# Reordering the head of a two-layer diffusion step: modulation blocks, first projection and first norm

## The chip, the core and the metric

The kernel runs on one core of one Trainium2 chip. The metric is the device time of one execution in microseconds (us); before the change it is 1575.97 us, the median of 3 runs (1575.73 to 1576.37).

## What is computed

One inference step of a hybrid diffusion backbone of two layers, with 128 context tokens and 128 latent tokens (256 columns together), model width 1024. Each layer is a SwiGLU feed-forward half step, a token mixer with three branches, and a second feed-forward half step. Only the very beginning matters here:

```
mod = silu(cond) @ w_ada + b_ada          # nine vectors of 1024 per layer and condition
h   = rmsnorm(x, gain) * (1 + scale) + shift
g,u = split(h @ w_in)                     # w_in: 1024 x 5632, width 2816 each
x   = x + 0.5 * gate * ((silu(g) * u) @ w_out)
```

Shift and scale are vectors 0 and 1 of `mod`. All numbers are fp32.

## The kernel before

Activations lie transposed: `x` is 8 chunks of 128 channels by 256 tokens. Every weight tile is 128 x 1024 fp32 (512 KB), loaded into a `raw` buffer (4 of them) by SyncE, cast on ScalarE to a high part (`emit_hi`, line 578; in the trace `wh`, or `big` for the first five tiles) and split on VectorE into a low part (`emit_lo`, line 588, raw minus high; `wl` or `big`). `split` (line 1681) does both for the next tile. `emit_lo` also asks for the next loads. One product of a 128 x 128 weight chunk k with an activation chunk k is three matmuls (high x high, high x low, low x high), called a triple here (`mm3`); eight triples k = 0 to 7 make one output tile. The first projection, feed-forward input of layer 0, takes 44 such tiles. Its first five (`T0 = 5`) are computed in the head, together with the modulation, because their activation operand comes chunk by chunk: three accumulate in the three `pm` buffers of PSUM and two in a spare one (`s` in the trace).

The activations are fed without the norm: `xfeed` (line 828) writes the high and low part of x times gain times (1 + scale) for one chunk, two instructions on ScalarE (`big<-x,amod`) and two on VectorE (`big<-x,amod,big`). The norm's factor per token is multiplied in after the projection, when a PSUM tile is evacuated: `wide<-pm,rb`, where `rb` holds the factor in all rows. It is formed from the sums of squares: `xstat` (line 765) squares a chunk on ScalarE and adds it to `sqa` on VectorE; `rstd_diag` (line 781) sums over partitions on TensorE, takes the power on GpSimd and builds a diagonal on VectorE; `rstd_rows` (line 795) spreads it with one fp32 product and copies it to `rb` on ScalarE. `norm_chain` (line 804) is the two in a row.

The modulation of the first norm comes in eight blocks, two loads of 512 KB each (`big<-wa`). Block b gives shift and scale of chunk b. `block_mm` (line 1699) multiplies silu(cond) with the block on TensorE (`pa<-big,silc`, 16 entries in the trace: the first 8 need the first half of the block, the others the second) and copies the result out on VectorE (`t1k<-pa`). `block_feed` (line 1709) turns that copy into columns on TensorE (`s<-cst,t1k`, 4 entries), adds bias and gain on VectorE (`mods`, `amod`, and two short writes of the shift), and calls `xfeed`.

Each engine works through its instructions in the order in which this Python program issues them. The head of before issues them so: loads of cT (8 KB), x (1 MB), cst and prm (about 130 KB each), then weight tiles 0 and 1, block 0, tile 2, block 1, tile 3, block 2, tile 4; all squares and the whole norm chain; `split` of two tiles; then ten steps. Step s issues `block_mm(s)`, the load of block s + 3, `block_feed(s - 1)`, then the triples of all chunks up to s - 2 for the tiles that have joined (`JOIN`: tiles 0 and 1 at step 2, then one each at steps 3, 4, 5), and a `split` where a tile is about to join. In the last steps high and low parts of tiles 5, 6 and the high part of tile 7 are issued (`AHEAD`, line 82). After the loop `ffn_in` (line 878) evacuates the five tiles and goes on with tile 5 into the first `pm` buffer that is free; its `end` issues the parts of further tiles (five ahead high, four ahead low) behind each evacuation.

Some later side work (the other modulation vectors) is issued by a planner, `Pace`, that predicts when each engine gets to what was issued; only the order of issue rests on it.

Of the kernel before, what the change touches and what calls it, by code (L numbers as in the profile page):

```python
# [17 lines left out]
D = 1024  # L18
# [22 lines left out]

ADA_DEPTH = 2
T0 = 5
JOIN = (0, 0, 3, 4, 5)
RAW_BUFS = 4
WH_BUFS = 5
WL_BUFS = 5
# [29 lines left out]
BR_LESS = (0, 0, 0, 0, 1, 1, 1, 1)  # L77
WO_LESS = (0, 0, 0, 0, 1, 1, 1, 1)
FO_LESS = (0, 0, 0, 0, 1, 1, 1)
LOADS = (2, 3, 4, 4)  # L80
PRE = 2
AHEAD = ("", "hl", "h", "lh", "")
T_SIDE = 3
T_SETUP = 6
YCUT = ((0, 2), (2, 2), (4, 2), (6, 2))
# [243 lines left out]


class Pace:
    """Predicts when each engine gets to what has been issued to it, so that side work can be issued where it waits for
    nothing. Only the order of issue rests on it; every wait is still placed by the tile framework."""

    LAT = {"pe": 0.25, "dve": 0.13, "act": 0.17, "pool": 0.2, "dma": 2.2}

# [91 lines left out]
def backbone(ctx: ExitStack, tc: tile.TileContext, seq, wst, wada, wa0, wrow, xT_d, cT_d, cB_d, ck_d, cv_d, h0_d, prm_d, cst_d,  # L428
# [117 lines left out]
    def settle(cond):  # L546
        idle = 0
        while not cond():
            cand = [(s, lst) for lst, n in ((side["first"], 99), (side["gens"], CONC), (side["slow"], 99)) for s in lst[:n]]
            cand = [c for c in sorted(cand, key=lambda c: when(c[0]) - FIRST * (c[1] is side["first"])) if when(c[0]) < 1e8]  # L550
            idle = 0 if any(step_side(*c) for c in cand) else idle + 1
            assert idle < 3
# [7 lines left out]
    def misc(gen):  # L560
        add(gen, True)
# [5 lines left out]
    def load(out, src):  # L567
        nc.sync.dma_start(out=out, in_=src)
        pace.op("dma", out.free_size() * P * 4 / 360e3, [out], [])

    def load_more(limit):
        while st["load"] < min(limit, st["cap"]):
            i = st["load"]
            raws[i] = pace.slot("raw", RAW_BUFS, wp.tile([P, 1024], F32, tag="raw", bufs=RAW_BUFS, name=nm("raw")))
            load(raws[i], wst[i])
            st["load"] += 1

    def emit_hi():
        u = st["hi"]
        if u < T0:  # L580
            hi = big(F32R)
        else:
            hi = pace.slot("wh", WH_BUFS, wp.tile([P, 1024], F32R, tag="wh", bufs=WH_BUFS, name=nm("wh")))
        S.copy(hi, raws[u])
        wt[u] = [hi, None]
        st["hi"] += 1
# [178 lines left out]
    def xstat(m):  # L765
        if m == 0:
            stat["acc"] = tmp("sqa", [P, NT], bufs=1)
            S.activation(out=stat["acc"], in_=x[:, 0], func=AF.Square)
            return lambda: None
        q = stat["sq"] = t1k()  # L770
        S.activation(out=q, in_=x[:, m], func=AF.Square)
        return lambda: V.tensor_tensor(out=stat["acc"], in0=stat["acc"], in1=q, op=ALU.add)
# [31 lines left out]
    def norm_chain(box):  # L804
        yield "pe", stat["acc"], "s1"
        dg = rstd_diag(stat["acc"], 1.0 / D)
        yield "pe", dg, "s1"
        box["rb"] = rstd_rows(dg)
# [856 lines left out]
        box["done"] = True  # L1665

    load(cT, cT_d)
    load(x, xT_d)
    load(cst[:, 0:CST_E], cst_d[:, 0:CST_E])
    load(prm[0], prm_d[0, :, 0:PRM_R])  # L1670
    V.memset(silc, 0.0)
    V.memset(halfc, -0.5)
    S.activation(out=silc[:, :, 0:2], in_=cT, func=AF.Silu)
# [7 lines left out]
    def split():  # L1681
        emit_hi()
        emit_lo()

    for n in LOADS[:-1]:
        load_more(n)
        block_load()
    load_more(LOADS[-1])
    feed_open(0, 0)
    for m in range(KD):  # L1690
        xstat(m)()
    box = {"rb": None}
    misc(norm_chain(box))
    split()
    split()
    settle(lambda: box["rb"] is not None)
    evs = {}

    def block_mm(b):
        ps = pada()  # L1700
        for k in range(KD):
            j = k % 4
            T_.matmul(ps[32 * j:32 * j + 32, :], lhsT=silc[:, k, :], rhs=blocks[b][k // 4][:, j * NT:(j + 1) * NT],
                      start=(k < 4), stop=(k >= 4))
        evs[b] = t1k()
        V.tensor_copy(evs[b], ps)
        blocks[b] = None
# [18 lines left out]
    spare = ps2()  # L1726
    pre, ws = [], []
    done = {}
    for step in range(KD + 2):
        if step < KD:  # L1730
            block_mm(step)
            if len(blocks) < KD:
                block_load()
                if len(blocks) == KD:
                    st["cap"] = len(seq)
                    load_more(st["lo"] + RAW_BUFS)
        if 1 <= step <= KD:
            block_feed(step - 1)
        for t in range(T0):
            if step < max(2, JOIN[t]):  # L1740
                continue
            if t == len(pre):
                ws.append(tiles8(use(("fin", 0, 0, (t % 2) * KF + t // 2))))
                pre.append(pmain(NT + 2) if t < 3 else spare[:, t - 3, 0:NT + 2])
                done[t] = 0
            while done[t] <= step - 2:
                k = done[t]
                mm3(pre[t], ws[t][k:k + 1], feed["hs"][k:k + 1], k == 0, k == KD - 1)
                done[t] += 1
        if st["lo"] < T0 and step + 2 >= JOIN[st["lo"]]:  # L1750
            split()
        if step >= KD - 3:
            for what in AHEAD[step - KD + 3]:
                what = emit_hi() if what == "h" else emit_lo()
    while st["lo"] < T0 + PRE:
        if st["hi"] == st["lo"]:
            emit_hi()
# [54 lines left out]
```

## Time and profile before

| | |
|---|---|
| median of 3 runs | 1575.97 us |
| profiled execution: span, its own time | 1579.0 us (the page gives no other time of it) |
| PE (TensorE) busy | 1547.9 us, 98% |
| DVE (VectorE) busy | 1313.5 us, 83% |
| ACT (ScalarE) busy | 877.7 us, 56% |
| POOL (GpSimd) busy | 58.7 us, 4% |
| transfers | 349.59 MB, mean 221 GB/s |

PE is the engine of the matmuls; its weight loads overlap. All times below are in us from the start of the span. A row of the timeline is start, duration, engine, line, operation, out<-in with buffer numbers left out, shapes and count; in brackets the idle time of the engine before it and what ended it. L397 is a helper through which all compute instructions are issued, so rows are told apart by their tiles.

### The profile page before, as it was taken

The numbers are of one execution on the slowest core, as the hardware profiler recorded it, in microseconds if no ns is written. First come the engines' busy times: TensorE is split into PE (matmuls) and PEld (weight loads), VectorE is DVE, ScalarE is ACT, GpSimd is POOL, SyncE is SP. The second block draws the span as 40 slices with busy tenths as digits, with TensorE's granted clock in tenths as the row PEclk, the third lists the DMA queues.
The fourth block names the chain that finished last, engine by engine and source line by source line (L and its number), as shares of the span: only waits on it lengthen the run. The fifth ranks groups of instructions, "written<-read, shape, count | busy, mean of one in ns | idle before, by whom it ended". The sixth has DMA issues, their size and how long they took to land.

```text
span 1579.0 us, 31076 instructions
## 1 busy us (share of the span) xinstructions
PE 1547.9 (98%) x12154; PEld 1449.6 (92%) x12154; DVE 1313.5 (83%) x2391; ACT 877.7 (56%) x1640; POOL 58.7 (4%) x65
## 2 busy tenths in 40 slices
PE   6999999999999999999999999999999999999997
PEld 4998889999979999899899998998998999999986
DVE  4777798988598997899989999898768889989754
ACT  3564447676467446644547544576746754665442
POOL 0000002000001100100001000100000010010000
PEclk9999999999999999999999999999999999999998
DMA  9698764553674666687765877555447457557652
GB/s 365 210 336 291 280 247 168 189 174 114 219 241 155 214 241 221 216 300 286 261 221 195 301 268 268 181 187 177 138 146 278 166 206 258 177 200 282 218 181 81
DMA packets 99171, 349.59 MB, mean 221 GB/s; under 512 B 10960, under 2 KB 14672, under 8 KB 98896
## 3 DMA queue, kind: packets, MB, share of 16 engines
q1 hardware_dynamic: 99024, 347.60, 62.4%
q8 instruction: 96, 1.57, 0.4%
q14 instruction: 51, 0.42, 0.1%
HBM read 343.36 MB, written 4.19 MB: 220 GB/s over the span
## 4 chain that ended last, share of the span: by engine, by line
PE 76%; issue 12%; DVE 7%; DMA 3%; ACT 1%; POOL 1%; DVEq 0%; SPq 0%; POOLq 0%; ACTq 0%
PE pm L397 67%; PE s L397 7%; DVE wl L397 2%; DVE big L397 2%; PE pa L397 2%; DMA big<-wada 2%; DVE t1k L397 1%; POOL osr L397 1%; DVE wide L397 0%; DMA t<-prm 0%; DMA x<-xT 0%; ACT big L397 0%; DVE sqa L397 0%; ACT L397 0%; ACT t1k L397 0%
## 5 line engine op out<-in xcount | busy, mean ns | idle before, releaser
L397 PE MATMUL pm<-big,wh 128*128 128x256 f32 (+2 forms) x6568 | 1288.8, 293 | 2.5 <-DVE wide L397 1.6
L397 PEld LDWEIGHTS pm<-big,wh 128*128 128x128 f32 x6568 | 1028.5, 189 | 46.3 <-issue 16.4
L397 PE MATMUL pm<-big,wl 128*128 128x256 f32 (+1 forms) x3592 | 1004.1, 281 | 0.0
L397 PEld LDWEIGHTS pm<-big,wl 128*128 128x128 f32 x3592 | 676.7, 188 | 2.4
L397 DVE TENSOR_TENSOR wl<-raw,wh 128x1024 fp32r<-128x1024 f32 x481 | 586.4, 1224 | 25.3 <-ACT wh L397 25.0
L397 ACT CAST wh<-raw 128x1024 fp32r<-128x1024 f32 x481 | 501.3, 1047 | 135.2 <-PE pm L397 105.4
L397 DVE SCALAR_TENSOR_TENSOR big<-big,big 128x1024 f32<-128x1024 f32 x198 | 241.4, 1219 | 9.7 <-DMA big<-wrow 8.6
L397 ACT CAST big<-t1k 128x256 fp32r<-128x256 f32 x88 | 35.8, 407 | 151.8 <-DVE t1k L397 151.8
L397 ACT ACTIVATE big<-x,amod 128x128 fp32r<-128x128 f32 x96 | 33.4, 396 | 100.9 <-DVE x L397 81.0
L397 PE MATMUL pm<-wh,big 128*128 128x512 f32 x256 | 88.5, 409 | 0.0
L397 DVE TENSOR_TENSOR wide<-pm,rb 128x258 f32<-128x258 f32 (+1 forms) x108 | 45.1, 421 | 39.2 <-PE pm L397 33.5
L397 DVE SCALAR_TENSOR_TENSOR x<-pm,mods,x 128x128 f32<-128x128 f32 x152 | 43.6, 343 | 37.1 <-PE pm L397 36.9
L397 ACT COPY big<-pm 128x256 f32<-128x256 f32 (+2 forms) x88 | 30.7, 372 | 59.2 <-PE pm L397 58.5
L397 PEld LDWEIGHTS pm<-wh,big 128*128 128x128 f32 x256 | 48.1, 188 | 13.2 <-issue 2.1
L397 DVE TENSOR_TENSOR big<-t1k,big 128x256 fp32r<-128x256 f32 x128 | 55.5, 438 | 1.6 <-ACT big L397 0.9
L397 ACT ACTIVATE t1k<-wide 128x128 f32<-128x128 f32 (+1 forms) x96 | 33.4, 395 | 38.3 <-DVE wide L397 38.2
L397 PE MATMUL s<-big,big 128*64 128x128 f32 (+4 forms) x528 | 51.4, 295 | 0.0
L397 PE MATMUL pm<-wl,big 128*128 128x512 f32 x128 | 50.4, 394 | 0.0
L397 ACT ACTIVATE t1k<-pm 128x256 f32<-128x256 f32 x58 | 22.3, 385 | 49.4 <-PE pm L397 49.4
L397 PEld LDWEIGHTS s<-big,big 128*64 128x64 f32 (+2 forms) x528 | 40.8, 163 | 5.9 <-issue 2.3
L397 DVE TENSOR_TENSOR big<-big,big 128x256 f32<-128x256 f32 (+1 forms) x64 | 39.9, 623 | 3.7 <-ACT big L397 2.3
L397 DVE SCALAR_TENSOR_TENSOR big<-big,cw,big 128x252 f32<-128x252 f32 (+1 forms) x96 | 39.2, 473 | 2.5 <-ACT big L397 2.5
(142 smaller groups left out, 1001.7 us busy)
## 6 DMA issues: line engine op xcount, KB each, us to landing
raw<-wst SPq DMA_DIRECT2D x486, 512.0 KB, 3.8
big<-wrow SPq DMA_DIRECT2D x96, 512.0 KB, 5.2
big<-wada SPq DMA_DIRECT2D x32, 512.0 KB, 5.8
big<-wa SPq DMA_DIRECT2D x16, 512.0 KB, 10.2
big<-cB SPq DMA_DIRECT2D x12, 512.0 KB, 7.0
big<-h SPq DMA_DIRECT2D x4, 512.0 KB, 4.7
x<-xT SPq DMA_DIRECT2D x1, 1024.0 KB, 6.0
ns<-t SPq DMA_DIRECT2D x8, 128.0 KB, 3.5
```

Source lines behind the costliest of these rows:

```text
L397: r = fn(*a, **k)
```

## The change

The first loads become cT, prm, cst, block 0, x, tile 0, block 1, tile 1, block 2. There is no norm chain ahead of the loop and no `split` ahead of it. The loop has nine steps. Step s issues `block_mm(s)`, the loads of tile s + 2 and block s + 3, then the triples of all chunks up to s - 1 for the first s tiles (at most five), then `block_feed(s)` of the same step, then (up to step 4) `split` of tile s, then the square and the addition of chunk s. High and low parts ahead: both of tile 5 at step 6, the high part of tile 6 at step 7, its low part at step 8. At step 8 `rstd_diag` is issued behind the triples of tile 1; `rstd_rows` follows the loop. A docstring is taken out.

```diff
-JOIN = (0, 0, 3, 4, 5)
-LOADS = (2, 3, 4, 4)
-AHEAD = ("", "hl", "h", "lh", "")
+AHEAD = {6: "hl", 7: "h", 8: "l"}
...
     load(cT, cT_d)
-    load(x, xT_d)
+    load(prm[0], prm_d[0, :, 0:PRM_R])
     load(cst[:, 0:CST_E], cst_d[:, 0:CST_E])
-    load(prm[0], prm_d[0, :, 0:PRM_R])
...
-    for n in LOADS[:-1]:
+    block_load()
+    load(x, xT_d)
+    for n in range(1, 3):
         load_more(n)
         block_load()
-    load_more(LOADS[-1])
     feed_open(0, 0)
-    for m in range(KD):
-        xstat(m)()
     box = {"rb": None}
-    misc(norm_chain(box))
-    split()
-    split()
-    settle(lambda: box["rb"] is not None)
...
-    for step in range(KD + 2):
+    for step in range(KD + 1):
         if step < KD:
             block_mm(step)
+            load_more(min(step + 3, T0))
...
-        if 1 <= step <= KD:
-            block_feed(step - 1)
-        for t in range(T0):
-            if step < max(2, JOIN[t]):
-                continue
+        for t in range(min(step, T0)):
...
-            while done[t] <= step - 2:
+            while done[t] < step:
                 k = done[t]
                 mm3(pre[t], ws[t][k:k + 1], feed["hs"][k:k + 1], k == 0, k == KD - 1)
                 done[t] += 1
-        if st["lo"] < T0 and step + 2 >= JOIN[st["lo"]]:
-            split()
-        if step >= KD - 3:
-            for what in AHEAD[step - KD + 3]:
-                what = emit_hi() if what == "h" else emit_lo()
+            if step == KD and t == 1:
+                dg = rstd_diag(stat["acc"], 1.0 / D)
+        if step < KD:
+            block_feed(step)
+            if step < T0:
+                split()
+            xstat(step)()
+        for what in AHEAD.get(step, ""):
+            what = emit_hi() if what == "h" else emit_lo()
+    box["rb"] = rstd_rows(dg)
```

## Rows read from the trace of the kernel before

**Rows 1.** Busy time by window, PE alone: window, length, busy (count), clock, DMA share, GB/s.

```profile
0.00:16.40 16.40, 2.14 (x6) 1.00 0.87 335
49.28:1569.00 1519.72, 1511.60 (x11864) 1.00 0.63 219
```

**Rows 2.** Chain of waits, 0 to 17 us: start, duration, what.

```profile
1.18 6.02 DMA x<-xT
```

**Rows 3.** Timeline of all engines, 0 to 60 us: the norm of the head.

```profile
7.97 3.61 DVE L397 TENSOR_TENSOR sqa<-sqa,t1k 128x256 f32<-128x256 f32 x7 [6.83 <-ACT t1k L397]
...
11.63 1.01 PE L397 MATMUL s<-cst,sqa 128*128 128x1 f32 x4 [11.63 <-DVE sqa L397]
...
13.77 0.15 DVE L397 TENSOR_SCALAR rsv<-s 128x2 f32<-128x2 f32 x1
...
15.27 1.22 PE L397 MATMUL s<-t1k,cst 128*128 128x256 f32 x2 [2.62 <-DVE rb L397]
...
16.53 0.37 ACT L397 COPY rb<-s 128x256 f32<-128x256 f32 x1 [4.74 <-PE s L397]
```

**Rows 4.** Busy time by window: PE, PEld, DVE, ACT, POOL, clock, DMA share, GB/s.

```profile
8.00:16.00 8.00, 1.74 (x6) 1.43 (x6) 5.78 (x13) 3.77 (x8) 0.70 (x1) 1.00 1.02 418
```

**Rows 5.** The loads of the blocks on SyncE's queue, by tile: starts, issue to landing.

```profile
L568 SPq DMA_DIRECT2D big<-wa x16: 327/328/711, 3.8 to 24.6; - x16
...
DMA to landing us min/median/max: 7.9/10.2/11.7
```

**Rows 6.** Timeline of PE, 9 to 30 us, and 38.5 to 43.2 us.

```profile
20.77 1.01 PE L397 MATMUL s<-cst,t1k 128*128 128x2 f32 x4
...
24.46 1.64 PE L397 MATMUL pm<-big,big 128*128 128x258 f32 x6
26.03 1.94 PE L397 MATMUL pa<-big,silc 128*32 128x256 f32 x16
...
28.52 1.69 PE L397 MATMUL pm<-big,big 128*128 128x258 f32 x12
...
38.47 1.07 PE L397 MATMUL pa<-big,silc 128*32 128x256 f32 x16
39.47 0.61 PE L397 MATMUL s<-cst,t1k 128*128 128x2 f32 x4
39.94 1.32 PE L397 MATMUL pm<-big,big 128*128 128x258 f32 x9
```

**Rows 7.** Timeline of DVE, then of ACT, 39.5 to 44.4 us: one step.

```profile
40.12 0.34 DVE L397 TENSOR_SCALAR mods<-s,prm 128x2 f32<-128x2 f32 x2
...
41.07 0.64 DVE L397 SCALAR_TENSOR_TENSOR big<-x,amod,big 128x128 fp32r<-128x128 f32 x2 [0.21 <-ACT big L397]
42.30 1.22 DVE L397 TENSOR_TENSOR wl<-raw,wh 128x1024 fp32r<-128x1024 f32 x1 [0.58 <-ACT wh L397]
43.44 0.41 DVE L397 COPY t1k<-pa 128x256 f32<-128x256 f32 x1
...
40.63 0.70 ACT L397 ACTIVATE big<-x,amod 128x128 fp32r<-128x128 f32 x2 [3.77 <-DVE amod L397]
41.23 1.03 ACT L397 CAST wh<-raw 128x1024 fp32r<-128x1024 f32 x1
```

**Rows 8.** Timeline of DVE, ACT and PE, 44 to 62 us: after the head.

```profile
48.44 0.42 DVE L397 TENSOR_TENSOR wide<-pm,rb 128x258 f32<-128x258 f32 x1
48.78 1.21 DVE L397 TENSOR_TENSOR wl<-raw,wh 128x1024 fp32r<-128x1024 f32 x1
50.62 1.23 DVE L397 TENSOR_TENSOR wl<-raw,wh 128x1024 fp32r<-128x1024 f32 x1 [0.63 <-ACT wh L397]
51.76 0.42 DVE L397 TENSOR_TENSOR wide<-pm,rb 128x258 f32<-128x258 f32 x1
...
48.95 0.70 ACT L397 ACTIVATE t1k<-wide 128x128 f32<-128x128 f32 x2 [1.01 <-DVE wide L397]
...
52.24 0.51 PE L397 MATMUL pm<-big,wh 128*128 128x258 f32 x2
```

## The prediction

> **What bounds the kernel now.** I read the busy windows first. From 49.28 us to 1569 us PE works 1511.60 of 1519.72 us [rows 1]: behind the head PE is the bound, so a microsecond by which PE starts the rest later or sooner is one in the end, and only 8.1 us of idle time there could take anything back. In the first 16.40 us PE works 2.14 us [rows 1]; that gap of 14.3 us is what the change is aimed at. The chain of waits and the timeline say what fills it: x lands at 7.20 [rows 2], seven additions run to 11.58, and the norm's steps follow until `rb` is written at 16.90 [rows 3]; block 0 waits behind them on PE's queue. From there to 49.28 PE has no gap worth naming, and it works slowly at first.
>
> PE's speed: the granted clock is printed as 1.00 for all these windows, but the same block product takes 1.94 us at 26.03 and 1.07 at 38.47, the column product 1.01 and 0.61, a matmul of a triple 0.27 (6 in 1.64) and then 0.14 or less (12 in 1.69) [rows 6]. So PE is at the lower level (1.2 GHz) until about 28.3 and at the upper (2.4 GHz) after, some 4 us after the first triples; before those it ran block and column products alone, at the lower level. A triple costs 0.8 us low, and 0.36 to 0.4 high (9 matmuls start over 1.1 us).
>
> **Part 1, the loads.** Up to block 7 the set of bytes is the same, only its order changes, so block 7 is in at 36.3 at the latest (issued 24.6, 11.7 more) as before [rows 5]. Transfers run at 418 GB/s [rows 4], 1.27 us per 512 KB. Block 0 takes x's place behind two tables of 0.26 MB (0.6 us): 7.20 + 0.7 = 7.9. Then x at 10.45, tile 0 at 11.7, block 1 at 14.25 (four more halves and tile 0), block 2 at 18.05, one block per 3.8 us after. SyncE meets one new buffer wait, tile 4 behind the release of tile 0's buffer (14.05 below), with blocks 5 to 7 queued behind it; it gets there only when block 2 lands, so I put nothing there. If that cover went, the blocks still have 6 us at the end. The Trainium skill, DMA: Bandwidth & Descriptors, Specifications, gives an HBM limit per core of about 358 GB/s; that speaks against this change, since block 1 would then come some 1.5 us later (an estimate by that page) and the end with it. The trace differs (418 GB/s [rows 4]), and it decides.
>
> **Part 2, the ring of a step.** Before, `block_feed(s - 1)` uses a copy made a step earlier, and the triples a chunk fed a step earlier still. After, the copy, column product, feed and triples of neighbouring steps are one ring, with VectorE in order. Count from the end of a column product. In the row of such a step that is 40.08 (39.47 + 0.61) [rows 6]. Feed's low part ends at 41.71, +1.63. ScalarE casts the next tile behind the feed (41.23 to 42.26), and the subtraction ends at 43.52, +3.45 [rows 7]. Up to step 4 that is there in every step, and behind it now the addition of squares, 0.44 [rows 3], +3.85, and only then the copy for the next column product, 0.42 [rows 7], +4.3. The column product is 0.6: the ring takes 4.95 us at the high rate, whatever PE does. Before, the distance of two column products in this stretch was about 3.6.
>
> Step by step, ends of the column product. **Step 0:** second half of block 0 at 7.9, half a block product 1.0, copy 0.45, column product 1.0: 10.4. Its subtraction ends at 14.05. **Step 1:** block 1 at 14.25, half a product 1.0, copy 0.45, one triple beside it, 1.0 behind: 17.0. **Step 2:** copy ends at 21.25, one triple of tile 0 beside it, two of tile 1 that wait for the subtraction (20.5) and end at 21.6 low, column product 1.0: 22.6. **Step 3** at the high rate: +4.4 for the last triples, +0.6: 27.6. **Step 4:** the new tile's four triples wait for the subtraction, +3.5, and end at +4.75: 32.9. **Step 5:** five such triples end at +5.15: 38.65. **Step 6**, no subtraction: feed +1.65, five triples to +3.25: 42.5, block 6 long there. **Step 7:** both parts of tile 5 now stand ahead of the copy, which ends at +4.2: 47.3. **Step 8:** feed +1.65, five triples (and the sums between them, 0.6): 51.2. Before, the five tiles end at 49.28.
>
> **Part 3, the norm.** The additions it removes from the front (7 x 0.44, [rows 3]) come back one per step, counted above. Its chain now lies behind the last addition, about 49.4: sums 0.6, then rsv to the product 1.5 (13.77 to 15.27 [rows 3]): 51.55. The low part of tile 6 stands there on VectorE ahead of the evacuation: 1.22 to 52.75. `rb` is ready a little sooner (51.55 + 0.6 to 0.7 + 0.4 = 52.6) and so costs nothing by itself; were the subtraction gone, it would be 52.6 all the same. The first evacuation, 0.42, ends at 53.15; before, at 48.86 [rows 8]. All `pm` buffers are full until then, so PE stands for 2 us that before had no place.
>
> **Part 4, high parts ahead.** Before, tile 7's high part was made in the head, so its subtraction followed the first evacuation at once (48.78) and the second evacuation ended at 52.18, when PE took the seventh tile (52.24) [rows 8]. Now that cast is issued behind the two activations of the first evacuation: 0.05 + 0.70 + 1.03 after 53.15, subtraction to 56.1, the next 1.15 to 57.25, evacuation 0.4: 57.65. PE has only tile 5 meanwhile (2.9 us), so it stands another 1.6.
>
> **Sum.** PE takes the seventh tile at 57.65 instead of 52.24: +5.4 us. The profiled span is 1579.0, 3.0 above the median; I carry the difference over, not the level: 1575.97 + 5.4 = 1581.4.
>
> **Bounds.** The clock's rise is not shown for such a mix. With the rise already before step 1's products (15 us) the steps lose their low costs where the ring shows them, 1.3 us: +4.1. With the rise only at 32, step 3 pays two triples' difference and its column product, 2.1 us more: +7.5. I take a rise during step 2 or 3, where triples stand among the products as they do in the last stretch before 28.3. The side work that the planner issues later is reordered a little; PE's 8.1 us of later waits bound a gain, and I allow 2 either way.
>
> **Rival A: the gap pays, faster.** If the subtraction does not hold the copy up (it is done while PE waits for a block, and the ring stays under the 3.8 us of three transfers), the transfers set the end: block 7 at 36.3, half a product 0.55, five triples 1.8, column product 0.6, feed 1.65, triples 1.8: 42.7; norm and evacuation 1.95 as above: 44.65 against 48.86; with part 4's delay the seventh tile starts at 49.15, -3.1, and -4.2 if ScalarE makes that cast early: 1571.8 to 1572.9. For it: 14.3 us of idle PE at the front. Against it: the order on VectorE in every step. The Trainium skill, Perfetto Trace Analysis, Optimization Strategy, advises finding the gaps of the bound engine and letting what they wait for start sooner; by that rule this rival holds. The trace agrees that the gap is there [rows 1], not that the work behind it can follow.
>
> **Rival B: no change.** The ring is as I say, but VectorE and ScalarE, rested by the pause, save 3 to 4 us of the later idle 8.1 [rows 1]: about 1578. Against it: that idle time is spread over 1520 us.
>
> **Rival C: PE stays slow.** Its gaps keep the low rate through step 4: that step pays seven triples at 0.45, a block product's 0.9 and 0.4 more, about 4.5, on top of the late bound: +10 to +12, 1586 to 1588. For it: the stretch of products without triples, 16.4 to 24.4, ran low throughout.
>
> That the change does not do what it says is partly true already: the norm does not form beside the projection but at its end, since the last square is the last step's; this is in part 3.
>
> **Chances.** My forecast 0.60, A 0.12, B 0.18, C 0.10. A measurement tells 0.2%, 3.15 us, from no change, so faster 0.12, same 0.18, slower 0.70. The range takes in the bounds of the clock (+4.1 to +7.5), 2 us of side work, most of B and the lower edge of C: 1576.5 to 1586.5; the forecast's own range is 1578 to 1585.
>
> **What would show it.** Block products begin at 6.7 to 8, not 16.4; column products end near 10, 17, 23, 28, 33, 39, 42.5, 47; the copy `t1k<-pa` starts right behind `sqa` on VectorE, and PE waits there. `wide<-pm,rb` first ends near 53, and PE has gaps of about 2 and 1.6 us there. I am wrong if column products follow each other in under 4 us, if PE has no gap between 49 and 58, or if PE's later idle time differs by more than 2 us.

## The result and the profile after

The changed kernel takes 1585.84 us (median of 6 runs, 1585.01 to 1587.14); the kernel before, on the same chip, 1576.17 (6 runs, 1575.37 to 1581.74). The ratio is 1.0057, 95% interval [1.0045, 1.007]: slower by 7.1 to 11.0 us, 9.7 by the medians. The forecast was slower by 5.4, to 1581.4. The direction held; the size forecast is little more than half of the one measured. The time lies in the stated range, 0.7 us below its upper end, and outside the forecast's own range of 1578 to 1585: the range reaches so far only because it took in the lower edge of rival C, whose mechanism is not what happened.

Busy time by window, PE alone (columns as in [rows 1]), of the changed kernel:

```profile
0.00:16.40 16.40, 5.54 (x37) 1.00 0.86 314
50.50:54.20 3.70, 3.23 (x16) 0.57 0.00 0
54.60:1574.00 1519.40, 1512.99 (x11861) 1.00 0.64 220
```

The first window answers to [rows 1]: PE now works 5.54 us of it, against 2.14. The gap at the front is partly filled, as the change says. The last window answers to the other row of [rows 1]: behind the head PE idles 6.4 us (1519.40 less 1512.99), against 8.1. So no wait behind the head brings the loss, and the timeline of PE of the changed kernel shows where it arises (start, duration, engine, line, what; idle time before and what ended it in brackets):

```profile
8.76 1.08 PE L395 MATMUL pa<-big,silc 128*32 128x256 f32 x8 [0.36 <-DMA big<-wa]
...
13.93 2.27 PE L395 MATMUL pa<-big,silc 128*32 128x256 f32 x16 [2.54 <-DMA big<-wa]
...
27.81 0.50 PE L395 MATMUL s<-cst,t1k 128*128 128x2 f32 x4
28.24 1.07 PE L395 MATMUL pa<-big,silc 128*32 128x256 f32 x16
...
33.12 0.50 PE L395 MATMUL s<-cst,t1k 128*128 128x2 f32 x4
...
34.92 1.64 PE L395 MATMUL pm<-big,big 128*128 128x258 f32 x9 [0.31 <-ACT big L395]
...
38.79 0.50 PE L395 MATMUL s<-cst,t1k 128*128 128x2 f32 x4
39.22 1.07 PE L395 MATMUL pa<-big,silc 128*32 128x256 f32 x16
...
47.42 0.61 PE L395 MATMUL s<-cst,t1k 128*128 128x2 f32 x4 [0.53 <-DVE t1k L395]
49.33 1.25 PE L395 MATMUL pm<-big,big 128*128 128x258 f32 x6 [1.30 <-ACT big L395]
...
51.38 1.49 PE L395 MATMUL s<-big,big 128*128 128x258 f32 x6
...
59.15 0.48 PE L395 MATMUL pm<-big,wh 128*128 128x258 f32 x2 [1.36 <-DVE wide L395]
```

Column products (`s<-cst,t1k`) end at 11.39, 17.79, 23.17, 28.31, 33.62, 39.29, 43.27 and 48.03; the prediction had 10.4, 17.0, 22.6, 27.6, 32.9, 38.65, 42.5 and 47.3. Each is 0.6 to 1.0 late, and the distances between them, which are the ring, agree within 0.3. The five tiles end at 52.87 (predicted 51.2), and the seventh tile starts at 59.15 (predicted 57.65; 52.24 in [rows 8]).

VectorE in one step of the changed kernel, timeline of DVE, against [rows 7]:

```profile
34.61 0.65 DVE L395 SCALAR_TENSOR_TENSOR big<-x,amod,big 128x128 fp32r<-128x128 f32 x2 [0.21 <-ACT big L395]
35.84 1.23 DVE L395 TENSOR_TENSOR big<-raw,big 128x1024 fp32r<-128x1024 f32 x1 [0.59 <-ACT big L395]
36.99 0.42 DVE L395 TENSOR_TENSOR sqa<-sqa,t1k 128x256 f32<-128x256 f32 x1
37.32 0.42 DVE L395 COPY t1k<-pa 128x256 f32<-128x256 f32 x1
...
54.17 0.43 DVE L395 TENSOR_TENSOR wide<-pm,rb 128x258 f32<-128x258 f32 x1 [0.60 <-ACT rb L395]
56.30 2.36 DVE L395 TENSOR_TENSOR wl<-raw,wh 128x1024 fp32r<-128x1024 f32 x2 [1.71 <-ACT wh L395]
```

The reader is to see one turn of the ring: the column product ends at 33.62, the feed's low part at 35.26 (+1.64; predicted 1.63), the subtraction at 37.07 (+3.45; 3.45), the addition of squares at 37.41 (+3.79; 3.85), the copy at 37.74 (+4.12; 4.3). The copy stands right behind `sqa`, and VectorE then waits 1.59 us for the next column product, which PE reaches behind the new tile's triples. So in this turn the copy is ready before PE asks for it. What PE waits for is the feed of the same step: 0.30 to 0.31 us for ScalarE in each of the steps 4 to 7, and once, at 31.81, 0.35 for the new tile's low part. It waits for the copy at steps 0 and 7 alone (0.55 and 0.53). At the end both evacuations wait for work that was late: the first for `rb`, 0.60 us after the subtraction is done (ends 54.60; predicted 53.15), the second behind the late cast of tile 7 (1.71 of waiting for ScalarE).

A figure of the Trainium skill was weighed in the prediction (DMA: Bandwidth & Descriptors, Specifications, about 358 GB/s per core). In the changed kernel too the trace differs: 412 GB/s from 8.00 to 16.00 us.

### The profile page after: what moved, and what is told of

Its sections match the earlier page's. It is cut to its first block, busy times and chain, and to the rows that moved or that the text cites. A ratio compares the mean times of both kernels' runs of the same rounds, so it can differ in the third digit from the quotient of the medians.

```text
span 1583.7 us, 31069 instructions
## 1 busy us (share of the span) xinstructions
PE 1553.9 (98%) x12154; PEld 1453.7 (92%) x12154; DVE 1314.4 (83%) x2391; ACT 879.5 (56%) x1640; POOL 58.7 (4%) x65
## 4 chain that ended last, share of the span: by engine, by line
PE 79%; issue 11%; DVE 6%; DMA 2%; ACT 1%; POOL 1%; SPq 0%; DVEq 0%; POOLq 0%
PE pm L395 70%; PE s L395 7%; DVE wl L395 2%; DVE big L395 2%; PE pa L395 1%; DVE t1k L395 1%; DMA big<-wa 1%; DMA big<-wada 1%; POOL osr L395 1%; ACT big L395 1%; DVE wide L395 0%; ACT wh L395 0%; ACT L395 0%; DVE x L395 0%; DVE mods L395 0%
## 5 line engine op out<-in xcount | busy, mean ns | idle before, releaser
L395 DVE SCALAR_TENSOR_TENSOR big<-big,big 128x1024 f32<-128x1024 f32 x198 | 241.9, 1222 | 10.4 <-DMA big<-wrow 8.9
L395 PE MATMUL s<-big,big 128*64 128x128 f32 (+4 forms) x528 | 52.4, 297 | 0.4 <-DVE big L395 0.4
L395 PE MATMUL pa<-big,silc 128*32 128x256 f32 x384 | 33.1, 430 | 10.9 <-DMA big<-wa 10.2
```

The lines of the kernel that those rows point to most:

```text
L395: r = fn(*a, **k)
```

## The experiments

Two numbers are kept apart for every kernel: when the seventh tile starts, and the rest of the span behind it (span less that start). Behind the head the compute instructions stand in the same order in all profiles. "Waits" is PE's idle time for the modulation weights of the later side work (`big<-wada`) in the profiled execution; the last column is a kernel's median less that of before on the same chip.

| kernel | ratio, 95% interval | seventh tile | rest | waits | median less before's |
|---|---|---|---|---|---|
| before, profile shown ahead | | 52.24 | 1526.8 | 3.4 | |
| before again | | 49.41 | 1523.5 | 0.5 | |
| before, third time | | 49.88 | 1524.8 | 2.4 | |
| changed | 1.0057 [1.0045, 1.007] | 59.15 | 1524.6 | 0.4 | +9.7 |
| changed once more | 1.0068 [1.0053, 1.0083] | 59.23 | 1527.2 | 1.7 | +10.8 |
| feed a step later | 1.005 [1.0035, 1.0065] | 54.10 | 1526.9 | 0.9 | +7.4 |
| norm early | 1.0045 [1.003, 1.006] | 56.14 | 1524.3 | 0.5 | +7.1 |
| tile 7's cast early | 1.0068 [1.0051, 1.0085] | 58.00 | 1526.4 | 1.2 | +10.2 |
| all three | 1.0028 [1.0018, 1.0039] | 53.95 | 1529.8 | 2.9 | +5.0 |
| x first | 1.0063 [1.0044, 1.0081] | 59.50 | 1524.6 | 0.2 | +10.8 |
| PE's last waits filled | 1.0077 [1.0057, 1.0097] | 58.07 | 1530.3 | 5.1 | +12.8 |
| before, with the ring alone | 1.0044 [1.003, 1.0057] | 57.63 | 1524.0 | 0.6 | +7.1 |
| before, PE kept busy at the front | 1.0013 [1.0004, 1.0023] | 51.38 | 1524.3 | 0.2 | +2.6 |
| new loads, no ring, norm and cast early | 1.0007 [0.9996, 1.0018] | 50.07 | 1526.3 | 1.8 | +1.1 |

### Is it the head at all?

By the two profiles at hand the seventh tile starts 6.9 us later (59.15 less 52.24), but the medians differ by 9.7. Either something behind the head costs 3 us, or the profile shown of before was a late one. The kernel before was profiled again, with no edit.

> The kernel before, profiled once more. Question: how much of the 9.7 us between the medians lies in the head, of which the two profiles show 6.9 (seventh tile at 59.15 instead of 52.24). Theory 1, the head carries it: the first profile of before was a long execution (span 1579.0, some 5 us over what its median leaves), with waits for big<-wada near 600 to 700 us that this one lacks; the span is near 1574 and the seventh tile begins at 50 to 52.3. Rival, the rest of the kernel carries part: the seventh tile begins at 52.2 again, and from there to the end this profile is over 2 us shorter than the 1524.5 us of the changed kernel.

PE's timeline of this second profile of before:

```profile
18.23 1.07 PE L397 MATMUL pa<-big,silc 128*32 128x256 f32 x16 [0.55 <-DVE t1k L397]
...
46.44 0.40 PE L397 MATMUL pm<-big,wh 128*128 128x258 f32 x2
...
49.41 0.51 PE L397 MATMUL pm<-big,wh 128*128 128x258 f32 x2
```

The seventh tile starts at 49.41, in a run of 1574.79 us with a span of 1572.9. The second block product takes 1.07 already at 18.23: TensorE is at its upper level 10 us sooner than in [rows 6], where 1.94 still stands at 26.03. A third profile, taken on another chip, was to tell which of the two is the usual one.

> The kernel before a third time, for where TensorE reaches the upper level and where the seventh tile begins. Theory 1: the rise lies between 17 and 29 us and the seventh tile between 49.3 and 52.3, later with a later rise. Rival: a seventh tile outside these, or no link between the two.

Its timeline of PE:

```profile
17.94 1.83 PE L397 MATMUL pa<-big,silc 128*32 128x256 f32 x16 [0.55 <-DVE t1k L397]
19.70 0.61 PE L397 MATMUL s<-cst,t1k 128*128 128x2 f32 x4
...
46.91 0.40 PE L397 MATMUL pm<-big,wh 128*128 128x258 f32 x2
...
49.88 0.51 PE L397 MATMUL pm<-big,wh 128*128 128x258 f32 x2
```

Here the level rises between 18 and 19.7, and the run takes 1576.71, about the median. So the profile shown was an unusual one: a run with its span takes about 1580.9 (1.9 us more, as in the second profile), and of the 52 times of before that were measured beside the other kernels four are longer. Of its 52.24, 2.4 to 2.8 us belong to that execution. From 49.41 and 49.88 the changed kernel's 59.15 is 9.3 to 9.7 later, as much as the difference of the medians.

The rest is not quite the same, though, even where PE does not wait. PE's busy time from the seventh tile to the end, for the changed kernel and for before the third time:

```profile
59.15:1583.70 1524.55, 1511.41 (x11844) 1.00 0.64 219
49.88:1574.70 1524.82, 1509.94 (x11845) 1.00 0.64 219
```

For the same instructions in the same order PE works 1509.9 to 1510.5 us in the three profiles of before, 1510.9 with the ring alone, and 1511.2 to 1513.3 in all others. So 1 to 3 us more can go behind the head in the other kernels, beside the waits of the table; the cause is open, and small differences between medians cannot be put down to the head alone.

The changed kernel was also profiled once more.

> The changed kernel once more, on the chip of the other runs of this call. Theory 1: the column products within 0.7 us of 11.4, 17.8, 23.2, 28.3, 33.6, 39.3, 43.3, 48.0, the seventh tile between 57.5 and 59.7, the time 8 to 11 us over before. Rival, the first profile of it was a special execution: a seventh tile before 57.

It starts the seventh tile at 59.23, and its ratio is 1.0068 [1.0053, 1.0083]: the end of the head repeats itself. The way there does not: from the third on, the column products end 0.9 to 1.2 us sooner than in the first profile (the last at 47.05 instead of 48.03), more than the 0.7 expected. Here the level rises sooner, with a block product of 1.07 at 22.07. What takes the advance back stands in the last section.

### The ring, taken out of the changed kernel

The feed goes one step later, as it was before, and the triples with it; everything else of the change stays.

```diff
-    for step in range(KD + 1):
+    for step in range(KD + 2):
...
-        for t in range(min(step, T0)):
+        if 1 <= step <= KD:
+            block_feed(step - 1)
+        for t in range(min(step - 1, T0)):
...
-            while done[t] < step:
+            while done[t] < step - 1:
...
-            if step == KD and t == 1:
+            if step == KD + 1 and t == 1:
...
-            block_feed(step)
```

> The changed kernel with its new load order, squares per step and norm at the end, but the column product and feed of a block one step later, as before, and the triples one chunk behind. Theory 1, the ring through VectorE paces the head: with a step of slack PE is the pace; the first column product moves from 11.4 to about 17.1 (it waits behind block 1), yet the last one comes near 44 instead of 48.0, the five tiles end near 48, the seventh tile begins at 54.5; 4 to 5 us faster than the changed kernel, still 3 to 5 slower than before (the norm's tail and the late cast stay). Rival, the load order or the squares between the steps cost the time: no more than 1 us faster than the changed kernel.

PE's timeline:

```profile
30.62 1.07 PE L395 MATMUL pa<-big,silc 128*32 128x256 f32 x16
...
39.70 1.07 PE L395 MATMUL pa<-big,silc 128*32 128x256 f32 x16
...
43.06 0.50 PE L395 MATMUL s<-cst,t1k 128*128 128x2 f32 x4
...
54.10 0.51 PE L395 MATMUL pm<-big,wh 128*128 128x258 f32 x2 [1.25 <-DVE wide L395]
```

The last column product ends at 43.56 instead of 48.03, the seventh tile starts 5.05 earlier, as expected. Two turns with the same work (two block products, two column products, 16 triples, all at the upper level) take 9.08 us here, from 30.62 to 39.70, and 10.98 in the changed kernel, from 28.24 to 39.22. PE's waits for the feed and for the new tile's low part are about half of that difference; the rest lies inside the groups of triples and was not broken down.

The time did not follow: a gain of 4 to 5 us was expected, the medians give 2.3 (+7.4 against +9.7), and the ratios, 1.0050 and 1.0057, have intervals that overlap. In this profile, the fastest of its four runs, the rest was 2.3 us longer than in that of the changed kernel, and PE worked 1512.8 us of it, 1.4 more. The ring is shown in the head; by the time alone it is not.

### The ring, put into the kernel before

The opposite edit: only the order of feed and triples is changed; loads, norm and casts ahead stay as they were before.

```diff
-    for step in range(KD + 2):
+    for step in range(KD + 1):
...
-        if 1 <= step <= KD:
-            block_feed(step - 1)
...
-            while done[t] <= step - 2:
+            while done[t] <= step - 1:
...
+        if step < KD:
+            block_feed(step)
```

> The kernel before with only the ring put in: the column product and feed of a block in the same step, behind the triples, and the triples one chunk further; its loads, norm at the front and high parts ahead stay as before (nine steps instead of ten). Theory 1, the ring alone costs most of it: column products follow each other at 4 to 4.8 us instead of 3.5, the last one comes near 48 (before: 43 to 46), the seventh tile begins between 53.5 and 56 (before: 49.4 and 52.2), and the time is 3 to 6 us over before. Rival, the ring is harmless without the squares and the new load order: the seventh tile begins before 52.3 and the time is within 1.5 us of before.

PE's timeline:

```profile
22.29 1.93 PE L397 MATMUL pa<-big,silc 128*32 128x256 f32 x16
...
27.29 1.07 PE L397 MATMUL pa<-big,silc 128*32 128x256 f32 x16
...
51.68 1.61 PE L397 MATMUL pm<-big,big 128*128 128x258 f32 x9 [1.30 <-ACT big L397]
...
57.63 0.48 PE L397 MATMUL pm<-big,wh 128*128 128x258 f32 x2 [0.26 <-DVE wide L397]
```

The eighth column product ends at 50.38, where about 48 was expected. The seventh tile starts 7.8 later than in the profile of before taken with it (49.88), and the time is 7.1 us longer, more than the 3 to 6 expected. Put into before, this one part of the change costs most of what the whole costs (10.8 on the same chip). Not all of the 7.8 need be the order of work: the level rises between 22.29 and 27.29 here, against 18 to 20 in the two usual profiles of before. Against the profile shown ahead, whose level rose at about 28, it is 5.4 later (52.24). Whether the new order delays the rise was not separated. The 1.30 us in which PE waits for ScalarE's feed behind the last column product is a wait that before had triples to fill.

### The norm's tail and the late cast

Norm early: two chunks are squared in each of the first four steps, so that the norm is done by step 6.

```diff
-            if step == KD and t == 1:
-                dg = rstd_diag(stat["acc"], 1.0 / D)
...
-            xstat(step)()
+            if step < KD // 2:
+                xstat(2 * step)()
+                xstat(2 * step + 1)()
+            if step == 5:
+                dg = rstd_diag(stat["acc"], 1.0 / D)
+            if step == 6:
+                box["rb"] = rstd_rows(dg)
...
-    box["rb"] = rstd_rows(dg)
```

> The changed kernel with two squares per step in steps 0 to 3 instead of one per step, the sums and power at the end of step 5 and the spread rows at the end of step 6, so that the norm is done before the last block. Theory 1: the ring stays as it is (last column product 48 to 48.6), the first evacuation ends near 52 instead of 54.60, the seventh tile begins near 56.5 to 57; 2 to 3 us faster than the changed kernel. Rival, the norm's tail is hidden behind the last tiles of the head anyway: the seventh tile stays within 0.7 of 59.15.

VectorE's timeline (the first evacuation), and then PE's:

```profile
51.17 0.42 DVE L395 TENSOR_TENSOR wide<-pm,rb 128x258 f32<-128x258 f32 x1
```

```profile
49.12 1.60 PE L395 MATMUL pm<-big,big 128*128 128x258 f32 x9 [1.30 <-ACT big L395]
...
56.14 0.48 PE L395 MATMUL pm<-big,wh 128*128 128x258 f32 x2 [1.35 <-DVE wide L395]
```

The first evacuation ends at 51.59 instead of 54.60 and the seventh tile starts 3.0 earlier, a little more than expected; the pause before it stays. Some 0.5 of it is not the norm's own: the clock does not fall here, and the filled waits (below) put the fall at that. The ratio is 1.0045 instead of 1.0057, with intervals that overlap.

Tile 7's cast early: its high part is issued in the loop again.

```diff
-AHEAD = {6: "hl", 7: "h", 8: "l"}
+AHEAD = {6: "hl", 7: "h", 8: "hl"}
```

> The changed kernel with the high part of tile 7 issued at step 8, as the kernel before had it ahead, nothing else changed. Theory 1: the pause of 1.36 us ahead of the seventh tile shrinks by about 1.1 (VectorE's subtraction no longer waits behind the two activations and the cast), the first evacuation stays near 54.6; 1.1 us faster than the changed kernel. Rival, the second evacuation is held by something else (the next cast, the raw tile's load): the pause stays within 0.3 of 1.36.

PE's timeline:

```profile
58.00 0.48 PE L395 MATMUL pm<-big,wh 128*128 128x258 f32 x2 [0.21 <-DVE wide L395]
```

The pause goes from 1.36 to 0.21 and the tile starts 1.15 earlier: the late cast is that wait. In the times (1.0068, interval [1.0051, 1.0085]) a gain of that size is not to be seen.

### What the early block brings

The two loads change places, with the ring kept.

```diff
+    load(x, xT_d)
     block_load()
-    load(x, xT_d)
```

> The changed kernel with x loaded ahead of block 0, as before, all else kept. Theory 1, block 0 is early for nothing, since the first step waits for block 1 anyway: the first column product comes 2.5 us later, the second at most 0.8 later, the seventh tile begins between 58.5 and 60; the time does not move by over 1 us. Rival, the early block is what the rest of the head stands on: all column products and the seventh tile come 2 us or more later.

PE's timeline:

```profile
12.00 1.01 PE L395 MATMUL s<-cst,t1k 128*128 128x2 f32 x4 [0.55 <-DVE t1k L395]
...
16.51 0.58 PE L395 MATMUL pm<-big,big 128*128 128x258 f32 x1 [0.46 <-DVE big L395]
16.89 0.97 PE L395 MATMUL s<-cst,t1k 128*128 128x2 f32 x4
```

The first column product ends 1.6 us later (13.01; 2.5 was expected), the second at 17.86 against 17.79: from then on nothing is left of the advance. In the changed kernel it is spent waiting 2.54 us for block 1; here block product 1 starts right behind the column product, at 13.03. The comparison is not clean: block product 1 ends 0.9 us sooner here than there (15.30 against 16.20), and 0.46 of that goes to a wait for tile 0's low part. The time is not told from that of the changed kernel.

### The clock

In the window 50.50 to 54.20 the changed kernel's granted clock is 0.57, behind two waits of PE of 0.53 and 1.30 us. Matmuls whose result nobody reads, into a spare PSUM tile, fill those two waits.

```diff
+    def filler(n):
+        pz = ps1(NT + 2)
+        for _ in range(n):
+            T_.matmul(pz, lhsT=ws[0][0][0], rhs=feed["hs"][0][0], start=True, stop=True)
+        drop("s1", pz)
...
+        if step == KD:
+            filler(10)
...
+        if step == KD - 1:
+            filler(4)
```

> The changed kernel with matmuls of no use in PE's two last waits: 4 ahead of the last column product, 10 ahead of the triples of the last chunk, into a PSUM tile that nobody reads. In the changed kernel the granted clock is 0.57 from 50.5 to 54.2 us, after PE's gaps, and the last 15 matmuls of the head take 0.2 to 0.27 us instead of 0.12. Theory 1, the gaps ahead bring that fall: with them filled no such row of 0.5 comes, the five triples of the last chunk take 1.9 instead of 3.5, the seventh tile begins 1.3 to 1.8 us sooner than 59.15. Rival, the fall comes from something else or costs nothing there: the seventh tile stays within 0.7 of 59.15.

PE's busy time by window, and its timeline:

```profile
50.50:54.20 3.70, 2.30 (x16) 1.00 0.08 14
```

```profile
46.84 0.61 PE L395 MATMUL s<-cst,t1k 128*128 128x2 f32 x4
...
58.07 0.48 PE L395 MATMUL pm<-big,wh 128*128 128x258 f32 x2 [1.35 <-DVE wide L395]
```

The clock stays at 1.00 and as many matmuls (16) take 2.30 instead of 3.23. The seventh tile starts at 58.07, 1.08 earlier; 1.3 to 1.8 was expected. More than half of that was there before the filled waits: the last column product ends at 47.45 instead of 48.03, and already the first one ends 0.7 sooner. From the last column product to the seventh tile it is 10.62 us here and 11.12 in the changed kernel, so about 0.5 is what the fall cost that execution. It acted through the norm: `rb`, for which the first evacuation waited 0.60, is ready in time here, and the evacuation starts behind the subtraction.

That the waits bring the fall is not shown. In the kernel with the norm early PE waits 0.47 and 1.30 us at the same two places and the clock stays at 1.00; with the ring alone in before it waits 0.22 and 1.30, and it stays too. The time with the waits filled was not shorter: 1.0077 [1.0057, 1.0097], an interval that overlaps with those of the changed kernel. In the profile the loss is in the rest (1530.3, with 5.1 us of waits for `big<-wada`); why is open.

At the front of the kernel before, such matmuls were to raise the clock sooner: 46 while the first loads run and 14 in the norm.

```diff
+    wf, wz = big(), big(F32R)
+    V.memset(wf[:, 0:P + NT], 0.5)
+    V.tensor_copy(wz[:, 0:P + NT], wf[:, 0:P + NT])
+    def warm(n):
+        pz = ps1(NT)
+        for _ in range(n):
+            T_.matmul(pz, lhsT=wz[:, 0:P], rhs=wz[:, P:P + NT], start=True, stop=True)
+        drop("s1", pz)
...
+    warm(46)
...
+        if box.pop("warm", None):
+            warm(14)
```

> The kernel before with matmuls of no use on TensorE while it waits at the front: 46 of 128x128 by 256 columns ahead of the norm's sums, 14 more between the sums and the spread rows, into a PSUM tile that nobody reads. Two profiles of before differ by 2.8 us in the head (seventh tile at 49.41 or 52.24), and in the first of them TensorE reaches the upper level only near 28 us, in the second near 18. Theory 1, the level of TensorE's clock at the front is worth that: every block product takes 1.07, the seventh tile begins near 49 and no later than 49.5 in every execution, 1 to 3 us faster than before. Rival, the level does not follow such work, or the blocks' arrival hides it: block products of 1.94 stay, the median does not move by 1 us.

PE's timeline:

```profile
14.90 1.07 PE L397 MATMUL pa<-big,silc 128*32 128x256 f32 x16
...
25.08 0.64 PE L397 MATMUL pa<-big,silc 128*32 128x256 f32 x8 [1.83 <-DMA big<-wa]
...
28.37 1.94 PE L397 MATMUL pa<-big,silc 128*32 128x256 f32 x16
```

A window of PE between:

```profile
26.50:30.00 3.50, 3.50 (x27) 0.55 1.03 414
```

The upper level is there at 14.90, and then PE waits for blocks (1.83 at 25.08), after which the clock is 0.55 and a block product takes 1.94 again. The seventh tile starts at 51.38, 1.5 to 2 later than in the usual profiles of before, and the time is 2.6 us longer by the medians. The expected gain is refuted. Of the rival, that the arrival of the blocks hides a faster PE, the mechanism is seen in this profile, but its number (no move of 1 us) failed as well. The profiled run, 1577.53, is the fastest of the twelve and no slower than the median of before (1577.39), so it does not show where the 2.6 us go. Its mean granted clock is 0.997; in eight of the other eleven it is 0.994, lower than in any of the 23 runs of before on that chip (0.995 to 0.998). A longer stretch at the lower level than the one seen here would fit that, but no profile shows it.

### Towards a better version

First the three repairs together (feed a step later, norm early, tile 7's cast early) on the changed kernel, with its order of loads.

> The changed kernel with its load order kept and the three other parts taken back together: feed one step later, norm done by step 6, high part of tile 7 ahead. Theory 1: with the ring, the norm's tail and the late cast gone, what is left is the load order and squares between the steps; the seventh tile begins near 52.4, first evacuation ends near 49.1; the time lies between before and 3 us above it. Rival, the parts do not add (the gain of one is taken by the next): the seventh tile comes after 53.5, the time stays over 4 us above before.

PE's timeline:

```profile
29.51 3.57 PE L395 MATMUL pm<-big,big 128*128 128x258 f32 x15
```

52.4 was expected, 53.95 came, and the time is 5.0 over before, where at most 3 was expected. Both are what the rival forecast (after 53.5, over 4): the gains of the parts do not add. Fifteen matmuls still take 3.57 at 29.51, 0.24 each: in this execution, the slowest of the twelve, the level rose only at about 33. What share of the missing gain is that late rise is not shown. The ratio is 1.0028 [1.0018, 1.0039]; about half of the loss is taken back.

The last version keeps the new loads and puts the feed of block s - 1 ahead of the block product s, as the first thing in a step, with the norm done by step 5.

```diff
-AHEAD = {6: "hl", 7: "h", 8: "l"}
+AHEAD = {6: "hl", 7: "h", 8: "lh"}
...
-    for step in range(KD + 1):
+    for step in range(KD + 2):
+        if 1 <= step <= KD:
+            block_feed(step - 1)
...
-        for t in range(min(step, T0)):
+        for t in range(min(step, T0) if step > 1 else 0):
...
-            while done[t] < step:
+            while done[t] < step - 1:
...
-            if step == KD and t == 1:
-                dg = rstd_diag(stat["acc"], 1.0 / D)
...
-            block_feed(step)
...
-            xstat(step)()
+            if step < KD // 2:
+                xstat(2 * step)()
+                xstat(2 * step + 1)()
+            if step == 4:
+                dg = rstd_diag(stat["acc"], 1.0 / D)
+            if step == 5:
+                box["rb"] = rstd_rows(dg)
...
-    box["rb"] = rstd_rows(dg)
```

> The changed kernel's load order with the head laid out anew: the column product of block s - 1 is issued ahead of block product s, the triples one chunk behind, squares two per step, the norm done by step 5, the high part of tile 7 ahead. No copy waits behind a subtraction that the same step needs. Theory 1: the seventh tile begins between 49.3 and 51.5, with little from the clock's level; the time is from 2 below to 2 above before. It beats before only where before reaches the upper level late. Rival, the gain of the earlier blocks comes through: over 2 us below before; or something else in the new load order costs: over 2 us above.

PE's timeline:

```profile
13.61 2.27 PE L395 MATMUL pa<-big,silc 128*32 128x256 f32 x16 [2.52 <-DMA big<-wa]
...
22.04 1.93 PE L395 MATMUL pa<-big,silc 128*32 128x256 f32 x16
...
28.30 0.64 PE L395 MATMUL pa<-big,silc 128*32 128x256 f32 x8 [1.23 <-DMA big<-wa]
...
50.07 0.49 PE L395 MATMUL pm<-big,wh 128*128 128x258 f32 x2
```

The first column product ends at 11.09, nearly 9 us before that of the second profile of before (19.84), and the eighth at 43.62, 0.7 behind its 42.91. The time is that of before (1.0007 [0.9996, 1.0018]). With feed, norm and tile 7's cast laid out anew nothing is lost, and the early start is worth nothing. The advance is spent in three places: PE waits 2.52 us for block 1, its block products still take 1.93 at 22.04, at the lower level, where the second profile of before has 1.07 from 18.23 on, and PE waits 1.23 for a block in the middle of the loop. No kernel of the study beats the one before.

## Why the prediction was right in direction and short in size

**What bounds it.** Right in the main. Over the table the time follows the start of the seventh tile roughly: the kernels that start it at 56 to 60 cost 7 to 11 us, the one that starts it at 50.07 costs nothing that can be told. Two do not fit. The kernel with the two waits filled costs 12.8 from 58.07, and the feed a step later costs 7.4 from 54.10; in both profiles the rest was longer.

**The sum: the step that fell short.** It is part 2. The five tiles were to end 1.9 later than before (51.2 less 49.28), and by the usual profiles they end 6.0 to 6.4 later (52.87 less 46.91 and 46.44). From there to the seventh tile the forecast held: 3.5 longer than before, and 3.3 measured (6.28 against 2.97). Most of the difference in part 2 is the base. "PE takes the seventh tile at 57.65 instead of 52.24: +5.4 us." and "I carry the difference over, not the level". The 52.24 was not what the kernel before usually does. The span, 1579.0, stood 3.0 above the median of the times, and the second profile shows that a run is 1.9 longer than its span (1574.79 and 1572.9): that execution was some 5 us above the median. The prediction saw the 3.0 and carried the difference of the heads over as if none of it lay in the head; 2.4 to 2.8 us lay in the head, 0.7 to 1.0 of it because x landed late (the norm's product on PE starts at 15.27 in [rows 3], at 14.60 and 14.31 in the other two profiles, with the same work ahead of it), the rest by the late rise of the clock. With the usual base the same working gives 57.65 less 49.4 to 49.9, +7.8 to +8.2. The row to ask was [rows 6]: a level that rose only at 28.3 was a trait of the execution, not of the kernel, and the prediction treated the clock as uncertain after the change alone. Its premise for the rise, triples among the products, does not come out either: in the other two profiles of before the level is up ahead of the first triples (21.32 and 21.80).

**The level after.** 59.15 against 57.65 is the other 1.5, in two terms. The column products are 0.7 late at step 7 (48.03 against 47.3): block 0's second half is taken by PE at 8.76 where 7.9 was predicted, and the "half a product" behind block 1 is a whole one, 2.27 at the lower level from 13.93. From there to the seventh tile 0.8 more is lost (11.12 against 10.35): about 0.5 of it goes with the fall of the clock, which was in no term. So 5.4, 2.4 to 2.8 of base and 1.5 make 9.3 to 9.7 in the head, and 9.7 was measured in the time. That the two meet is in part luck, since the rest varies by more than the difference.

**The ring.** The distances of the column products came out as predicted, and both edits of it alone (5.05 out of the changed head, 7.8 into the head of before) show that the order of feed and triples costs the head several us. How it costs them was right in part. "PE waits there", at the copy behind `sqa`, holds at steps 0 and 7; in the steps between PE waits for the feed, and the copy is ready before the triples end, as the prediction's own steps 4 and 5 had it (+4.75 and +5.15 against +4.3). That the subtraction and the addition on VectorE are the costly part was not tried by itself. The expectation of the second edit was too low: it left out that PE has nothing to do behind the last feed (1.30), and its last column product came 2.4 late before that.

**The norm's tail, the late cast.** Right in the main. "`rb` is ready a little sooner", and so costs nothing by itself, did not hold: the evacuation waited 0.60 for it, under the fallen clock; with the clock up it did not. First evacuation 53.15 predicted, 54.60 measured, late with the steps ahead of it. The pauses of PE came out at 0.92 and 1.36 where 2 and 1.6 were predicted; the first was smaller because the five tiles ended at 52.87 instead of 51.2, partly under the fallen clock.

**The loads.** In the prediction's steps, step 1 waits for block 1 whatever block 0 does, and the run with x first fits: the second column product ends at the same time.

**Rival A** fell by the ring. Its own number was too hopeful in another way as well: the last version above starts the seventh tile at 50.07, near the 49.15 that it gave, but this is no gain on 49.4 to 49.9. The rule beside it (the Trainium skill, Perfetto Trace Analysis, Optimization Strategy: find the gaps of the bound engine and let what they wait for start sooner) was followed to the letter, and PE's busy time in the first 16.40 us rose from 2.14 to 5.54; the traces show that it pays only as far as the work behind the gap can follow. **Rival B** fell: PE's idle time behind the head is 1.7 less than before (6.4 against 8.1), where 3 to 4 were needed, and the rest of the span (1524.6) lies between those of the other two profiles of before (1523.5 and 1524.8). **Rival C** fell, though its 1586 to 1588 is next to the time measured: the fourth column product takes 0.50, so the upper level is there by 27.81.

**Readings.** Three are off, with little weight. An addition of 0.44 is not what [rows 3] give (3.61 for seven); single ones take 0.42 in the changed kernel. 512 KB at 418 GB/s are 1.25 us, not 1.27. And the sign of being wrong, column products "in under 4 us", was broken by the prediction's own step 6 (3.85; 3.98 was measured), so it could not tell anything.

## What to carry to other kernels

Before tightening a software pipeline by a step, write down one turn of it in program order on the engine that is in it twice or more: here one step of slack hid the feed of a chunk behind PE's other work, and without it two turns with the same work took 10.98 us instead of 9.08. A load moved to the front is worth nothing when the next stage waits for a load that has not moved; look for the first wait behind it. A head of 50 us should be judged from several profiles of the kernel before, and a span that stands above the median is to be searched for its excess inside the stretch that the change touches, before the difference is carried over.

## What was not expected of the hardware

TensorE's rise to its upper level came, in the same kernel with the same order of work, at 18, at about 19 and at 28 us in three profiles; ahead of it stand in all three the norm's product and one or more block products with a gap of 0.55 between them. In the ten profiles with the new loads or the ring the first block product of 1.07 us, or half of one in 0.64, comes between 22 and 33 us, in none as early as in the two usual ones of before. Whether the change delays the rise, and what that costs, was not tried by itself.

The fall at the end of the changed head came behind waits of 0.53 and 1.30 us, but the same two places with waits of 0.47 and 1.30 had no fall in the kernel with the norm early, so these waits do not settle it. In one profile the fall shows as 0.57 over 3.7 us; in the second, in this window of PE of the changed kernel once more, the granted clock is 0.50, the lower level, for 10 us, though PE works 8.73 of them:

```profile
48.00:58.00 10.00, 8.73 (x36) 0.50 0.24 82
```

```profile
46.44 0.61 PE L395 MATMUL s<-cst,t1k 128*128 128x2 f32 x4 [0.51 <-DVE t1k L395]
...
59.23 0.48 PE L395 MATMUL pm<-big,wh 128*128 128x258 f32 x2
```

It cost more there: from the last column product (47.05) to the seventh tile it is 12.18 us, against 11.12 in the first profile and 10.62 with the clock up. The advance of 0.98 with which that execution came to its last column product is gone by the seventh tile, which PE reaches without a wait.

Behind the head, with the same order of instructions, the rest took from 1523.5 to 1530.3 us over the profiles, and 0.2 to 5.1 us of it PE waits for `big<-wada`. That spread is larger than the gain of one repaired wait (1.15 us for the late cast), which is why the repairs are read from the head's own rows. What decides how late those loads land was not tried and stays open.
